# Weight buffers given out by hand, a pair's last product in another place, gates multiplied in two turns, and spilled values read into their own tiles, in a two-layer encoder kernel

## The chip, the cores and the metric

The kernel runs on one core of one Trainium2 chip. The metric is device time in microseconds (us) of one execution of the whole program: the median of three runs, beside one further execution that the hardware profiler recorded.

## What is computed

The reference is a two-layer encoder trunk in fp32 (512 frames of 1024 features). Cut to what matters:

```python
for i in range(2):
    h = rmsnorm(x, norm1_g[i])
    z = h @ w_in[i] + b_in[i]                       # 1024 x 12296, cut into q/k/v/gates
    # branch A: 4 mLSTM heads (dk = dv = 256), q/k through a causal conv and silu
    # branch B: 4 retention heads (dk = 256, dv = 512), rotary q/k, a decay per head
    y_m = sigmoid(mo) * head_layernorm(mlstm(...))
    y_r = silu(rg) * head_layernorm(retention(...))
    merged = sigmoid(gm) * (y_m @ w_bm[i]) + sigmoid(gr) * (y_r @ w_br[i])
    x = x + merged @ w_out[i]
    x = x + square(relu(rmsnorm(x, norm2_g[i]) @ w_ff1[i] + b_ff1[i])) @ w_ff2[i] + b_ff2[i]
    x = x + sigmoid(rmsnorm(x, norm3_g[i]) @ w_pe_gate[i]) * (p[i] @ w_pe[i])
return rmsnorm(x, final_g)
```

## The kernel before

**Number format and matmuls.** Activations are held transposed, features on the 128 partitions and the 512 frames along the free axis. Every operand is split into a high and a low part (`split`, L285): ScalarE (ACT) copies the fp32 value into the reduced format, VectorE (DVE) subtracts that copy from the value. A product of two operands is three TensorE (PE) matmuls: high by high, high by low, low by high. So each weight block of 128x1024 values costs one DMA into a raw buffer (`wr`), one ACT copy (`wh`, L286) and one DVE subtraction (`wl`, L287) before PE can use it.

**Units.** The weights come as one list of units in a fixed order (`unit_list`, L151). A `T8` unit is one 1024x128 block (24 matmuls of 512 columns, `t8`, L446). A `V` unit is a block of a value projection. `PE` units are the two halves of the embedding weights (24 matmuls each, L1443). A `PAIR` is a 1024x256 block that is multiplied with seven products of quarter-size blocks instead of eight (`run_pair`, L472); a `WIDE` is the same for the retention values (`run_wide`, L508). The layer runs through the mLSTM heads, the retention heads 0 to 3, the branch outputs, `w_out`, the first and second feed-forward product (`ff1`, `ff2`, L1363 and L1391) and the gated embedding.

**A pair's seven products.** P1, P5, P6, P2, P3, P7 and P4 are twelve matmuls of 256 columns each. They use three PSUM banks: P1, P6, P7 and P4 are accumulated one after the other in bank `a`, P5 and P3 in bank `c`, P2 in bank `b`. After each product the bank is read out (`done`), by ACT or DVE in `pair_tiles` (L541), by DVE additions into the residual `x` in `ff2` (L1400). P6 can't begin before P1's reading of bank `a` is over, P7 not before P6's, and P4 not before P7's. The weights of a pair are four pieces: A (P1, P5), C (P3, P7), B (P6, P2) and D (P4); D is formed on DVE from the raw pieces (L421 and L424). The last product, P4, is not issued with the other six: it is put into a list `later`, and `flush` (L467) issues it inside the next piece of work. In `run_pair` that is after the next pair's P1 and P5 (L503), in `t8` after half of the block (L454), and there are calls in `scores` (L757), in `attend` (L785) and in `r_out` (L1109). P4's reading then starts what hangs on the pair (`consume`): rotary for the queries and keys, silu for the gates.

**Raw buffers.** There are four raw buffers of one pool tag (`RAWS`, L57), handed out in turn by the pool, and one more in the layer's `low` pool, which is used while units before `w_out` are loaded (`fill_raws`, L362). A raw A piece is kept until C has been split, because D needs both. SyncE (SP) issues the loads in the order of the units.

**Norms.** A norm collects its sum of squares in one tile (`ssum`, L631) and spreads the reciprocal root over the partitions in another (`rb`, L703); both are 512 values wide and sit in the pool `one`.

**Retention heads.** `rv_vals` (L1152) computes the values of two heads at once; those of the second head are written to DRAM. `rv_load` (L1192) brings them back: GpSimd (POOL) issues four loads of 256 KB into temporary tiles (six of them turn round), and ACT and DVE split each into the head's value tiles. `r_gates` (L1091) computes two of a head's four gate tiles as one pair; `r_out` (L1100) transposes the head's output in four steps of four matmuls (`back`, L799) and multiplies each by its gate. `back` needs the scaled output of the head, and the multiplication needs the gate's silu.

**What sets the order.** The program is written in the order above, but a scheduler reorders the instructions within each engine by its own estimate of when operands are ready. So the order on PE is not always that of the code; the order of the built programs was compared for this text. Two kinds of instruction keep the written order: the splits of the weights on ACT and DVE, and the loads on SP. POOL's queue also carries 1 MB DRAM-to-DRAM sums of weight blocks (`step`, L326), each tied to a matmul as a pace.

In the names of the trace `l0r2o1` is layer 0, retention head 2, the second pair of gates; `brq` and `brk` are queries and keys; `l0o31` is block 3, column pair 1 of `ff2` in layer 0; a last letter a, b or c is the PSUM bank.

Of the kernel before, what the change touches and what calls it, by code (L numbers as in the profile page):

```python
# [42 lines left out]
P = 128  # L43
# [191 lines left out]

def build(ctx, tc, ins, out):
# [118 lines left out]
    room = unit_list(0).index(("T8", "w_out", 0, 0))  # L355
    cur["room"], cur["more"] = (), None

# [3 lines left out]

    def fill_raws(most=RAWS + 1):  # L362
        while at["load"] < len(loads) and len(raws) + len(kept) < most:
            n, x = loads[at["load"]]
            r = None
            if n in cur["room"] and cur["more"] not in raws:
                cur["more"] = n, x
                r = cur["low"].tile([P, UN], F32, name=f"wr{at['load']}", tag="wrx", bufs=1)
            elif len(raws) - (cur["more"] in raws) >= RAWS:
# [20 lines left out]
    def prep_next():  # L390
        n, x = order[at["prep"]]
        at["prep"] += 1
        fill_raws()

        w = Q if x == "D" else UN
# [21 lines left out]
        if x == "A" or wide and x[0] == "t2":  # L417
            kept[n, x] = r
        elif x == "C":

            ve.tensor_tensor(raws[n, "B"][:, Q:], kept.pop((n, "A"))[:, Q:], r[:, :Q], OP.add)  # L421
        elif x == "B":

            ve.tensor_tensor(r[:, :Q], r[:, :Q], r[:, Q:], OP.add)  # L424
            formed[n, "D"] = r
        elif wide and x[0] == "B21":
            t = cur["br"].tile([P, UN], F32, name=f"t4{n}_{x[1]}", tag=("ph", "pl")[x[1]])
            ve.tensor_tensor(t, kept.pop((n, ("t2", x[1]))), r, OP.add)
            formed[n, ("t4", x[1])] = t

    def ready(k):
# [39 lines left out]

    def run_pair(name, act, done):  # L472

# [66 lines left out]

    def pair_tiles(name, act, consume, y=None):  # L541

        y = y or [tmp(f"{name}y{d}") for d in range(2)]
        a, b = slice(0, S), slice(S, T)
# [17 lines left out]

        run_pair(name, act, done)

# [37 lines left out]
    class Norm:  # L602


        def __init__(self, name, i, gain, act=None, j0=0, j1=NT):
# [20 lines left out]
        def square(self, k, x, add=None):  # L626
            w = self.n * P
            x = x[:, self.s]
            if self.sum is None:
                pl = cur["last"] if self.half else opool  # L630
                sq = pl.tile([P, w if self.half else T], F32, name=f"{self.name}sum", tag="ssum", bufs=1)[:, :w]  # L631
            else:
# [57 lines left out]
        def spread(self):  # L690
# [10 lines left out]
            te.matmul(o[:, :w], ones_r, dl, start=False, stop=True)  # L701
            pl = cur["last"] if self.half else opool
            self.b = pl.tile([P, w if self.half else T], F32, name=f"{n}rb", tag="rb", bufs=1)[:, :w]  # L703
            ac.activation(self.b, o[:, :w], AF.Copy)
# [71 lines left out]
    def attend(nm, pt, vh, vl, c0, n, num):  # L776
        ph, pl, offs = pt
        for j in range(NT):
# [121 lines left out]
    cur["tmp"], cur["ntmp"] = cur["low"], NTMP  # L900
    cur["room"] = range(room)
    n1 = Norm("l0n1", 0, "g1", acts(xa_pool, "l0n1"))
# [16 lines left out]
    for i in range(L):  # L919
        act_side, ph_side = ("right", "left") if i == 0 else ("left", "right")  # L920
        xa = n1.act
        if i:
            cur["low"] = phase(f"low{i}", ph_side)
            cur["tmp"], cur["ntmp"] = cur["low"], NTMP
            cur["room"] = range(i * NU // L, i * NU // L + room)
        cur["br"] = phase(f"br{i}", ph_side)
# [163 lines left out]

        def r_gates(h, w, gs):  # L1091

# [4 lines left out]

            pair_tiles(f"l{i}r{h}o{w}", xs, consume)

        def r_out(h, num, y, gs=None):  # L1100
            nm = f"l{i}r{h}o"
            if gs is None:
                gs = {}
                r_gates(h, 0, gs)
            r_gates(h, 1, gs)
            for v in range(4):
                o = back(nm, num, v)
                if v == 0:
                    flush()  # L1109
                ve.scalar_tensor_tensor(gs[v], o, bcol(i, "grn", 4 * h + v), gs[v], OP.mult, OP.mult)  # L1110
                split(gs[v], y[0][(4 * h) % 8 + v], y[1][(4 * h) % 8 + v])

        def gm_gates(p):
# [77 lines left out]

        def rv_load(h):  # L1192

            v = value_tiles(f"l{i}r{h}")
            for j in range(NT):
                t = tmp(f"l{i}r{h}vr{j}")
                gp.dma_start(t, rv_dram[i, h // 2, j])
                split(t, v[0][j][:, :T], v[1][j][:, :T])
            return v

        ym = acts(cur["br"], f"l{i}ym")
# [189 lines left out]
        def ff2(b, p):  # L1391
# [10 lines left out]
            def done(x_, o):  # L1402
# [35 lines left out]
        n3_pool = phase(f"n3{i}", act_side)  # L1438
        n3 = Norm(f"l{i}n3", i, "g3", acts(n3_pool, f"l{i}n3"))


        pe = n3_pool.tile([P, KT, T], F32, name=f"l{i}pe", tag="pe")
        for u in range(2):  # L1443
            _, wh, wl = unit("PE")
            for c in range(4):
                o = ps(f"l{i}pe{u}{c}")
                for k in range(2):
                    s = slice((2 * c + k) * P, (2 * c + k + 1) * P)
                    mm3(o, wh[:, s], wl[:, s], pth[:, k, :], ptl[:, k, :], k == 0, k == 1)
                ac.activation(pe[:, 4 * u + c, :], o, AF.Copy)  # L1450
        for _, b, p in rest:
            ff2(b, p)
        flush()
        shift(cur["ff"], ph_side, False)
# [9 lines left out]
        nn = ([Norm(f"l{i}n4{a}", i, "gf", None, 2 * a, 2 * a + 2) for a in range(2)] if last  # L1464
              else [Norm(f"l{i + 1}n1", i + 1, "g1", acts(xa_pool, f"l{i + 1}n1"))])

# [203 lines left out]
```

## Time and profile before

| | us |
|---|---|
| median of three runs (lowest, highest) | 2348.12 (2347.74, 2348.28) |
| the profiled execution's own time | 2347.49 |
| its span, first to last instruction | 2345.8 |
| ScalarE (ACT) busy | 1218.9 |
| GpSimd (POOL) busy | 245.7 |
| DMA: bytes moved | 394.89 MB |

PE is busy for almost the whole span, so the table alone says little. The views that do are the one of waits (who waited for whom, with the length of each wait), the timeline (each instruction with its start, its duration, and in brackets the idle time of its engine before it and what ended that) and the one of one tile. A PE duration in the timeline is that of one matmul from its first to its last step; matmuls overlap, so the pace is read from one start to the next.

### The profile page before, as it was taken

Reading aid. Unit: us, or ns where it says so; the run is one execution under the profiler, and the core shown is the slowest. Engines: PE = TensorE matmul, PEld = TensorE weight load, DVE = VectorE, ACT = ScalarE, POOL = GpSimd, SP = SyncE. Lnnn points to the kernel's source line nnn. Section 1 sums busy time; section 2 is a strip of 40 time slices with the busy share of each in tenths; the row PEclk is TensorE's granted clock in tenths of the full one; section 3 lists DMA queues with packets and bytes.
Section 4 is the critical chain, followed back from the end, with each engine's and each line's share of the span. In section 5 each row is a group of like instructions: output and inputs, shape, how many; then the busy total and the mean of one; then the engine's idle time right before and its main releaser. Section 6 shows DMA issues by size and latency. Waiting matters only on the chain. (4 is left out here: it accounts for less than half of the span.)

```text
span 2345.8 us, 35261 instructions
## 1 busy us (share of the span) xinstructions
PE 2320.2 (99%) x13660; PEld 2056.2 (88%) x13660; DVE 1722.9 (73%) x2658; ACT 1218.9 (52%) x1768; POOL 245.7 (10%) x369
## 2 busy tenths in 40 slices
PE   9999999999999999999999999999999999999998
PEld 7888899898898898899888888998989988998997
DVE  7878767895675577677878787778958656776785
ACT  6656444553554445446557564454536445445454
POOL 3111101100102100000321110000000020000012
PEclk9999999999999999999999999999999999999999
DMA  5666676667578667676775645434343542433431
GB/s 201 187 180 172 218 229 170 205 189 202 168 230 269 195 198 189 199 219 181 206 221 169 182 124 186 136 126 158 108 158 104 166 153 96 130 108 98 132 117 59
DMA packets 146631, 394.89 MB, mean 168 GB/s; under 512 B 15376, under 2 KB 18832, under 8 KB 146464
## 3 DMA queue, kind: packets, MB, share of 16 engines
q1 hardware_dynamic: 99952, 247.77, 32.0%
q0 software_dynamic: 31104, 117.45, 20.4%
q10 hardware_dynamic: 15408, 27.43, 3.3%
q8 instruction: 107, 1.75, 0.3%
q14 instruction: 60, 0.49, 0.1%
HBM read 373.71 MB, written 123.73 MB: 212 GB/s over the span
## 5 line engine op out<-in xcount | busy, mean ns | idle before, releaser
L286 ACT ACTIVATE wh<-wr 128x1024 fp32r<-128x1024 f32 (+1 forms) x223 | 232.2, 1044 | 276.5 <-issue 69.6
L287 DVE TENSOR_TENSOR wl<-wr,wh 128x1024 fp32r<-128x1024 f32 (+1 forms) x221 | 271.9, 1232 | 77.7 <-ACT wh L286 77.5
L286 ACT ACTIVATE wh_B<-wr 128x1024 fp32r<-128x1024 f32 x100 | 105.9, 1059 | 159.2 <-PE l0f L443 8.5
L287 DVE TENSOR_TENSOR wl_B<-wr,wh_B 128x1024 fp32r<-128x1024 f32 x100 | 121.9, 1219 | 32.5 <-ACT wh_B L286 32.3
L286 ACT ACTIVATE wh_D<-wr 128x512 fp32r<-128x512 f32 x76 | 48.0, 632 | 124.9 <-DVE wr L424 65.4
L286 ACT ACTIVATE wh_C<-wr 128x1024 fp32r<-128x1024 f32 x76 | 80.2, 1056 | 61.3 <-issue 9.2
L286 ACT ACTIVATE wh_A<-wr 128x1024 fp32r<-128x1024 f32 x76 | 79.9, 1052 | 54.7 <-PE l1f L443 9.0
L287 DVE TENSOR_TENSOR wl_C<-wr,wh_C 128x1024 fp32r<-128x1024 f32 x76 | 94.3, 1240 | 18.7 <-ACT wh_C L286 18.5
L287 DVE TENSOR_TENSOR wl_A<-wr,wh_A 128x1024 fp32r<-128x1024 f32 x76 | 92.7, 1220 | 17.3 <-ACT wh_A L286 17.3
L442 PE MATMUL l1f<-l1n2h,wh 128*128 128x512 f32 x256 | 99.8, 390 | 0.0
L442 PE MATMUL l0f<-l0n2h,wh 128*128 128x512 f32 x256 | 99.8, 390 | 0.0
L444 PE MATMUL l0f<-l0n2h,wl 128*128 128x512 f32 x256 | 99.7, 389 | 0.0
L444 PE MATMUL l1f<-l1n2h,wl 128*128 128x512 f32 x256 | 99.7, 389 | 0.0
L443 PE MATMUL l1f<-l1n2l,wh 128*128 128x512 f32 x256 | 99.6, 389 | 0.0
L443 PE MATMUL l0f<-l0n2l,wh 128*128 128x512 f32 x256 | 99.6, 389 | 0.0
L287 DVE TENSOR_TENSOR wl_D<-wr,wh_D 128x512 fp32r<-128x512 f32 x76 | 52.4, 689 | 33.2 <-ACT wh_D L286 31.7
L421 DVE TENSOR_TENSOR wr<-wr,wr 128x512 f32<-128x512 f32 x76 | 52.1, 686 | 14.6 <-DMA wr<-wpairs 13.1
L444 PEld LDWEIGHTS l0f<-l0n2h,wl 128*128 128x128 f32 x256 | 48.0, 188 | 10.2
L444 PEld LDWEIGHTS l1f<-l1n2h,wl 128*128 128x128 f32 x256 | 48.1, 188 | 10.1
L443 PEld LDWEIGHTS l1f<-l1n2l,wh 128*128 128x128 f32 x256 | 48.1, 188 | 9.8
L442 PEld LDWEIGHTS l0f<-l0n2h,wh 128*128 128x128 f32 x256 | 48.1, 188 | 9.8
L442 PEld LDWEIGHTS l1f<-l1n2h,wh 128*128 128x128 f32 x256 | 48.1, 188 | 9.7
(5625 smaller groups left out, 8357.9 us busy)
## 6 DMA issues: line engine op xcount, KB each, us to landing
wr<-wstream SPq DMA_DIRECT2D x219, 512.0 KB, 4.2
wr<-wpairs SPq DMA_DIRECT2D x228, 256.0 KB, 2.8
wr<-wwide SPq DMA_DIRECT2D x24, 512.0 KB, 4.0
s0t<-wwide POOLq DMA_DIRECT2D x5, 1024.0 KB, 7.8
s4t<-wwide POOLq DMA_DIRECT2D x5, 1024.0 KB, 9.0
s12t<-wwide POOLq DMA_DIRECT2D x5, 1024.0 KB, 8.1
s16t<-wwide POOLq DMA_DIRECT2D x5, 1024.0 KB, 8.5
s1t<-wpairs POOLq DMA_DIRECT2D x4, 1024.0 KB, 6.7
```

The source lines that it names most:

```text
L286: a = ac.activation(hi_ap, src, AF.Copy)
L287: return a, ve.tensor_sub(lo_ap, src, hi_ap.bitcast(F32))
L421: ve.tensor_tensor(raws[n, "B"][:, Q:], kept.pop((n, "A"))[:, Q:], r[:, :Q], OP.add)
L442: te.matmul(o, sh, mh, start=first, stop=False)
L443: te.matmul(o, sh, ml, start=False, stop=False)
L444: cur["mm"] = te.matmul(o, sl, mh, start=False, stop=last)
```

## The change

Four things are changed.

1. `fill_raws` keeps its own list of free raw buffers. Each has a name and a tag of its own, is taken by a load when it is free, and goes back to the list when the split (or the forming of D) that reads it last has been issued. Beside the four and the one in `low` there is a sixth, `one`: the two norm tiles become one tile `nr` of 1024 values, sum in the first half and spread root in the second, and loads from the unit `WIDE rv0` up to `w_out` may use that tile.
2. `run_pair` calls `flush` after P6 instead of after P5, except in one pair (`early`). The `flush` in `scores` goes, that in `attend` comes after the second block instead of the first. One of the two embedding units is moved behind the last four pairs of `ff2`, with a `flush` in its third block. In `ff2` the norm's `tile3` for the first column tile of a pair is called after P3 instead of P6.
3. `r_out` transposes and multiplies gates 0 and 1 inside the second gate pair (after its P2), transposes 2 and 3 after it, and puts their multiplications into `later`, behind the P4 they need.
4. `rv_load` becomes `rv_fetch`, which loads straight into the low halves of the head's value tiles before the next head's pairs, and `rv_split`, which splits them in place after the scores.

```diff
@@ unit_list
     pairs(ff_order()[0])
     u.append(("PE", 0))
+    pairs(ff_order()[1])
     u.append(("PE", 1))
-    pairs(ff_order()[1])
@@ build
-    cur["room"], cur["more"] = (), None
+    wide0 = unit_list(0).index(("WIDE", (0, "rv0"), 0))
+    where = {n + i * NU // L: ("low", "one") if n >= wide0 else ("low",) for i in range(L) for n in range(room)}
+    free, taken = ["low", "one"] + list(range(RAWS)), {}
+    def norm_tile():
+        return opool.tile([P, 2 * T], F32, name="nr", tag="nr", bufs=1)
+    def raw_tile(a):
+        if a == "one":
+            return norm_tile()
+        pl, tag = (cur["low"], "wrx") if a == "low" else (wpool, f"wr{a}")
+        return pl.tile([P, UN], F32, name=f"wr{at['load']}", tag=tag, bufs=1)
...
+            fits = where.get(n, ()) if n * L // NU == cur["layer"] else ()
+            a = next((a for a in free if a in range(RAWS) or a in fits), None)
+            if a is None:
                 break
-            raws[n, x] = r = r or wpool.tile([P, UN], F32, name=f"wr{at['load']}", tag="wr", bufs=RAWS)
+            free.remove(a)
+            taken[n, x] = a
+            raws[n, x] = r = raw_tile(a)
...
+        def give(*a):
+            free.extend(taken.pop(k) for k in a)
@@ run_pair
-        product("P1")
-        product("P5")
-        flush()
-        for x in ("P6", "P2", "P3", "P7"):
+        for x in ("P1", "P5", "P6", "P2", "P3", "P7"):
             product(x)
+            if x == ("P5" if early else "P6"):
+                flush()
+            if x == "P2" and mid:
+                mid()
         later.append(last)
@@ scores
-        flush()
@@ attend
-            if j == 0:
+            if j == 1:
                 flush()
@@ r_out
-            r_gates(h, 1, gs)
-            for v in range(4):
-                o = back(nm, num, v)
-                if v == 0:
-                    flush()
+            def gate(v, o):
                 ve.scalar_tensor_tensor(gs[v], o, bcol(i, "grn", 4 * h + v), gs[v], OP.mult, OP.mult)
                 split(gs[v], y[0][(4 * h) % 8 + v], y[1][(4 * h) % 8 + v])
+            def turn(a):
+                return [(v, back(nm, num, v)) for v in (a, a + 1)]
+            r_gates(h, 1, gs, mid=lambda: [gate(*t) for t in turn(0)])
+            o = turn(2)
+            later.insert(0, lambda: [gate(*t) for t in o])
@@ rv_load -> rv_fetch, rv_split
-                t = tmp(f"l{i}r{h}vr{j}")
-                gp.dma_start(t, rv_dram[i, h // 2, j])
-                split(t, v[0][j][:, :T], v[1][j][:, :T])
+                gp.dma_start(v[1][j][:, :T].bitcast(F32), rv_dram[i, h // 2, j])
             return v
+        def rv_split(v):
+            for hi, lo in zip(*v):
+                split(lo[:, :T].bitcast(F32), hi[:, :T], lo[:, :T])
@@ order of the retention heads
         num = r_attend(0, pt, vv)
+        vv = rv_fetch(1)
         gs = {}
         r_gates(0, 0, gs)
-        vv = rv_load(1)
         pt = r_scores(1, qk)
+        rv_split(vv)
...
-        r_gates(1, 0, gs)
+        r_gates(1, 0, gs, early=True)
...
         num = r_attend(2, pt, vv)
+        vv = rv_fetch(3)
         qk = r_qk(3)
...
-        vv = rv_load(3)
         pt = r_scores(3, qk)
+        rv_split(vv)
@@ ff2 and the embedding
-                if b == 3 and p and x_ in ("P6", "P7"):
+                if b == 3 and p and x_ in ("P3", "P7"):
...
+        embed(0)
         for _, b, p in rest:
             ff2(b, p)
-        flush()
+        embed(1)
```

More of the change, by code (lines that the diff above doesn't have):

```diff
@@ L355, in build, with fill_raws @@
     room = unit_list(0).index(("T8", "w_out", 0, 0))
[L356 removed]
+    wide0 = unit_list(0).index(("WIDE", (0, "rv0"), 0))
[8 more added lines that the diff above has]
+        return pl.tile([P, UN], F32, name=f"wr{at['load']}", tag=tag, bufs=1)
     def halves(n):
         return [slice(0, Q), slice(Q, UN)] if n == 1 else [slice(0, UN)]
[L362 to L363 removed]
+    def fill_raws(most=None):
+        while at["load"] < len(loads) and at["load"] != most:
             n, x = loads[at["load"]]
[L365 to L369, printed above, removed]
+            fits = where.get(n, ()) if n * L // NU == cur["layer"] else ()
+            a = next((a for a in free if a in range(RAWS) or a in fits), None)
+            if a is None:
                 break
[L371 removed]
+            free.remove(a)
+            taken[n, x] = a
+            raws[n, x] = r = raw_tile(a)
             if x:
@@ L539, in run_wide, with pair_tiles @@
                     done(x, t, bank[b][t])
-    def pair_tiles(name, act, consume, y=None):
-        y = y or [tmp(f"{name}y{d}") for d in range(2)]
+    def pair_tiles(name, act, consume, **kw):
+        y = [tmp(f"{name}y{d}") for d in range(2)]
         a, b = slice(0, S), slice(S, T)
@@ L629, in square @@
             if self.sum is None:
-                pl = cur["last"] if self.half else opool
-                sq = pl.tile([P, w if self.half else T], F32, name=f"{self.name}sum", tag="ssum", bufs=1)[:, :w]
+                if self.half:
+                    sq = cur["last"].tile([P, w], F32, name=f"{self.name}sum", tag="ssum", bufs=1)
+                else:
+                    self.own = self.own or norm_tile()
+                    sq = self.own[:, 0:w]
             else:
@@ L701, in spread @@
             te.matmul(o[:, :w], ones_r, dl, start=False, stop=True)
-            pl = cur["last"] if self.half else opool
-            self.b = pl.tile([P, w if self.half else T], F32, name=f"{n}rb", tag="rb", bufs=1)[:, :w]
+            self.b = self.own[:, T:T + w]
             ac.activation(self.b, o[:, :w], AF.Copy)
@@ L900, in build @@
     cur["tmp"], cur["ntmp"] = cur["low"], NTMP
-    cur["room"] = range(room)
+    cur["layer"] = 0
     n1 = Norm("l0n1", 0, "g1", acts(xa_pool, "l0n1"))
@@ L924, in build @@
             cur["tmp"], cur["ntmp"] = cur["low"], NTMP
-            cur["room"] = range(i * NU // L, i * NU // L + room)
+            cur["layer"] = i
         cur["br"] = phase(f"br{i}", ph_side)
@@ L1089, in r_attend, with r_gates @@
             return num
-        def r_gates(h, w, gs):
+        def r_gates(h, w, gs, **kw):
             def consume(g):
@@ L1438, in build, with embed @@
         n3_pool = phase(f"n3{i}", act_side)
-        n3 = Norm(f"l{i}n3", i, "g3", acts(n3_pool, f"l{i}n3"))
+        n3 = Norm(f"l{i}n3", i, "g3", acts(n3_pool, f"l{i}n3"), own=n2.own)
         pe = n3_pool.tile([P, KT, T], F32, name=f"l{i}pe", tag="pe")
-        for u in range(2):
+        def embed(u):
             _, wh, wl = unit("PE")
@@ L1463, in build @@
         cur["tmp"], cur["ntmp"] = phase(f"pg{i}", ph_side), 7
-        nn = ([Norm(f"l{i}n4{a}", i, "gf", None, 2 * a, 2 * a + 2) for a in range(2)] if last
-              else [Norm(f"l{i + 1}n1", i + 1, "g1", acts(xa_pool, f"l{i + 1}n1"))])
+        nn = ([Norm(f"l{i}n4{a}", i, "gf", None, 2 * a, 2 * a + 2, n3.own) for a in range(2)] if last
+              else [Norm(f"l{i + 1}n1", i + 1, "g1", acts(xa_pool, f"l{i + 1}n1"), own=n3.own)])
         def pe_evac(o, c, s, nn):
```

19 lines of the change are left out of this document (14 added, 5 removed).

## The prediction

> **What bounds the kernel now.** First the page: its first part, then the view of stages for one stretch.
>
> ```profile
> span 2345.8 us, 35261 instructions
> PE 2320.2 (99%) x13660; PEld 2056.2 (88%) x13660; DVE 1722.9 (73%) x2658; ACT 1218.9 (52%) x1768; POOL 245.7 (10%) x369
> ...
> 600.00:660.00 60.00, 56.02 (x422) 53.85 (x421) 46.13 (x75) 37.26 (x63) 2.88 (x4) 0.94 0.50 158
> ```
>
> PE is busy for 2320.2 of 2345.8 us. The change takes no matmul away and adds none, so it can only win what PE loses: 25.6 us of idle time at most, plus time in which matmuls run slowly. Of the stretches of 60 us that I read, the one from 600 stands out inside the kernel: 56.02 us busy, and a granted clock (the last column but two) of 0.94. So the next view is what PE waited for.
>
> ```profile
> PE l0r2o1a L491 <- ACT wh_A L286: 3.4, 1, 3.4
> PE l1o33a L491 <- DVE l1x L1400: 1.6, 1, 1.6
> PE l0o33a L491 <- DVE l0x L1400: 1.3, 1, 1.3
> ...
> PE l0r0o0a L491 <- DVE l0r0o0y L558: 1.2, 1, 1.2
> PE l1r0o0a L491 <- DVE l1r0o0y L558: 1.2, 1, 1.2
> ...
> PE l0r1brqa L491 <- DVE l0r1brqy L558: 1.0, 1, 1.0
> ...
> PE l0o12a L491 <- DVE l0x L1400: 0.7, 1, 0.7
> ...
> PE l1r2o0a L491 <- ACT l1r2o0y L548: 0.5, 1, 0.5
> ...
> PE l0r2o0a L491 <- ACT l0r2o0y L548: 0.4, 1, 0.4
> PE l1r2o1a L491 <- DVE l1r2o1y L558: 0.3, 1, 0.3
> PE l0r2o1a L491 <- DVE l0r2o1y L558: 0.2, 1, 0.2
> ```
>
> There are few waits, each with one place. I sort them by the edit that touches them. Seven are a P4 that waits for P7's reading of bank a by DVE: the two o33, the two r0o0, r1brq and the two r2o1 (6.8 us). Three belong to the values read back in front of r2o0 (3.4 + 0.4 + 0.5 = 4.3 us). The rows left out belong to the first projection, to r0's values and to both ends of the kernel, places where both programs have the same order; they stay, as does the wait at o12, which is a P6.
>
> **What the large wait costs.** The timeline of PE, then of ACT, around it:
>
> ```profile
> 599.98 0.28 PE L492 MATMUL l0r2o0b<-l0xnl,wh_B 128*128 128x256 f32 x1
> 600.10 0.28 PE L493 MATMUL l0r2o0b<-l0xnh,wl_B 128*128 128x256 f32 x1
> 603.78 0.58 PE L491 MATMUL l0r2o1a<-l0xnh,wh_A 128*128 128x256 f32 x1 [3.40 <-ACT wh_A L286]
> ...
> 604.38 0.41 PE L491 MATMUL l0r2o1c<-l0xsh,wh_A 128*128 128x256 f32 x1
> 604.59 0.41 PE L492 MATMUL l0r2o1c<-l0xsl,wh_A 128*128 128x256 f32 x1
> ...
> 609.15 0.33 PE L493 MATMUL l0r2o0c<-l0xsh,wl_C 128*128 128x256 f32 x1
> ```
> ```profile
> 601.16 0.63 ACT L286 ACTIVATE l0r3vh<-l0r3vr 128x512 fp32r<-128x512 f32 x1 [0.48 <-DMA l0r3vr<-rv_spill]
> 602.16 0.63 ACT L286 ACTIVATE l0r3vh<-l0r3vr 128x512 fp32r<-128x512 f32 x1 [0.37 <-DMA l0r3vr<-rv_spill]
> 602.69 1.04 ACT L286 ACTIVATE wh_A<-wr 128x1024 fp32r<-128x1024 f32 x1
> 604.95 0.36 ACT L548 ACTIVATE l0r2o0y<-l0r2o0a 128x256 f32<-128x256 f32 x1
> ```
>
> Matmuls of 256 columns start 0.12 us apart (599.98, 600.10). From 600.10 to 603.78 there are 3.68 us, 3.56 more than that step, so a wait costs 0.16 more than its row says. After it the step is 0.21 (604.38, 604.59) up to 609.15: 5.4 us, less r2o0's wait of 0.4 + 0.16, hold some 23 matmuls that each lose 0.09, 2.1 us. The cause is on ACT: the weight split wh_A that PE needs stands behind value splits that wait for their DMA.
>
> **The sum: what goes.** Part 4 takes the value splits out of this place: in the built program they stand on ACT right behind the outputs of head 2, ahead of the branch output's 192 matmuls (44 us at 0.23 a matmul, two fences on), and the splits of r2o0's weights follow each other. 4.3 us of waits, 3 x 0.16, and 2.1 of slow clock: 6.9 us. Part 2 puts more work between P7 and P4: P6 of the next pair (1.4 us at 0.12 a matmul) for r1brq, the next pair's P1 and P5 for r0o0, attend blocks for r2o1, and 18 embedding matmuls for o33 (4 us). Each is longer than the wait it covers. 6.8 us and 7 x 0.16: 7.9 us. Together 14.8 us.
>
> **What comes, 1: values split earlier.** rv_fetch(1) issues its loads as head 0's value tiles come free, and in the built order two of the four splits stand on ACT ahead of head 0's last output, the third ahead of a key split and of P1's reading in r0o0. The nearest rows are the same loads of before:
>
> ```profile
> 402.92 0.39 PE L444 MATMUL l0r0a<-l0r0vh,l0r0pl 128*128 128x512 f32 x1
> 403.15 0.28 PE L491 MATMUL l0r0o0a<-l0xnh,wh_A 128*128 128x256 f32 x1
> ```
> ```profile
> 405.16 1.27 POOL L1197 DMA_DIRECT2D l0r1vr<-rv_spill  x2 [20.78 <-DVE l0r0mv L792]
> ...
> 408.59 0.59 POOL L1197 DMA_DIRECT2D l0r1vr<-rv_spill  x1
> ...
> 411.51 0.63 ACT L286 ACTIVATE l0r1vh<-l0r1vr 128x512 fp32r<-128x512 f32 x1 [0.41 <-DMA l0r1vr<-rv_spill]
> ```
> ```profile
> DMA to landing us min/median/max: 2.9/3.4/3.7
> ...
> DMA to landing us min/median/max: 4.4/11.1/12.1
> ```
>
> The last two lines are from the views of the tiles l0r1vr and l0r3vr. From issue (408.59) to the waiting split (411.51) there are 2.9 us; I take 3.0. The third tile is read last by the 26th of 30 attend matmuls, which starts four steps of 0.23 before the last (402.0) and ends 0.39 later; issue 402.45, landing 405.45, split to 406.0, key split to 406.55, P1's reading (0.4) to 407.0, P6 at 407.15. PE would come to P6 at 403.15 + 24 x 0.12 and three interleaved matmuls, 406.45. That is 0.7 us late, in two layers: 1.4. Bounds: 0 if the landing is 0.7 us shorter, and 2 x 1.5 with the median landing of 3.4 and both splits behind it; 11 us is a rival below. At head 3 only two splits stand ahead of P1's reading, and the same count ends before P6: 0. The Trainium skill, "DMA: Bandwidth & Descriptors", section "Anatomy of one DMA — SWDGE (gpsimd) path", puts one such transfer at about 2.0 us fixed plus bytes over 436 GB/s, an estimate of 2.6 us for 256 KB. The rows here are above it; by the rule this item would be 0.6 instead of 1.4.
>
> **What comes, 2: P6 in P4's place.** P6 lost the cover that P4 gave it; it waits for P1's reading. In `pair_tiles` ACT reads within 0.5 us and PE needs 1.4 for P5, so nothing is due. In `ff2` the reading is on DVE, behind wl_B. The DVE timeline at o12 and at o32, then PE with the P1 and P6 starts of o32:
>
> ```profile
> 942.25 1.23 DVE L287 TENSOR_TENSOR wl_B<-wr,wh_B 128x1024 fp32r<-128x1024 f32 x1 [2.78 <-ACT wh_B L286]
> 943.39 0.41 DVE L1400 TENSOR_TENSOR l0x<-l0x,l0o12a 128x256 f32<-128x256 f32 x1
> ...
> 1108.35 0.41 DVE L1400 TENSOR_TENSOR l0x<-l0x,l0o31a 128x256 f32<-128x256 f32 x1
> ...
> 1109.28 1.21 DVE L287 TENSOR_TENSOR wl_B<-wr,wh_B 128x1024 fp32r<-128x1024 f32 x1
> 1110.42 0.40 DVE L1400 TENSOR_TENSOR l0x<-l0x,l0o32a 128x256 f32<-128x256 f32 x1
> ```
> ```profile
> 1088.11 0.39 PE L444 MATMUL l0pe<-l0pth,wl 128*128 128x512 f32 x1
> 1088.33 0.28 PE L491 MATMUL l0o30a<-l0hh,wh_A 128*128 128x256 f32 x1
> ...
> 1106.73 0.28 PE L491 MATMUL l0o32a<-l0hh,wh_A 128*128 128x256 f32 x1
> ...
> 1110.97 0.35 PE L491 MATMUL l0o32a<-l0hh,wh_B 128*128 128x256 f32 x1
> ```
>
> P6 starts 4.24 us after P1, and its bank was read 4.09 after P1: just in time. The built order puts seven of P4's twelve matmuls ahead of P6 here, so P6 comes up at 24 + 7 matmuls after P1, 3.67 us, and waits 0.57 for DVE, which goes from P7's reading of o31 to P1's of o32 without a pause. The same for o33, and in layer 1: 2.3 us. I worked the other twenty pairs that have a P4 in front in the same way from their rows. In the pairs 01, 11 and 21 the order leaves P4 first, nothing. At o12 in layer 0 wl_B is late (DVE sat idle 2.78 us for wh_B) and PE waits 0.7 already; with two of P4's matmuls in front instead of twelve it comes 1.2 earlier and waits that much more. o22 there 0.8; the rest 0.5 in all. o31 would wait 0.9 in each layer, but there the built order moves the addition for D, which waited for a DMA, behind the reading; nothing. With half of the embedding gone from the front, o30's hidden tiles have 5.5 us instead of 11; the splits of before end in time, wl_B follows 0.3 late: 0.6 for both layers. Together 5.4 us. Bounds: 0 if DVE's new order makes the readings earlier by as much, 12 if every P6 waits as late as its reading was, with credit only for the pairs 01, 11 and 21.
>
> **What comes, 3: nothing.** The sixth raw buffer and the handing out cost no instruction; `ff2` still has four. Loads come earlier in the retention part, where no wait of PE names one. Shared norm tile: its readers and the loads are far apart. Two-turn gating moves transposes, 16 per head, without adding any; gates 2 and 3 come one P4 later and are used in the branch output, behind 48 matmuls of 0.12 and 18 of 0.23, 9.9 us. Were that cover gone, PE would wait there once per layer for two gate operations and two splits, by the rows of such sizes above 0.6 us each, 2.4.
>
> The sum: -14.8 + 1.4 + 5.4 = -8.0. The profiled execution took 2347.5 us (span 2345.8), so 2339.5; the median of before lies 0.6 higher, which gives **2340.1**.
>
> The Trainium skill, "TensorE: Matmul & The Clock Gate", section "Part 1: The HAM clock gate", says the array falls to half rate after an idle window of about 3.4 us and comes back after about as long a busy one. The trace agrees with the first: of the waits only the one of 3.4 us is followed by slow steps. By the second the slow stretch would cost 1.7 us instead of 2.1, and the sum would be -7.6.
>
> **The rivals.**
> - *Nothing new waits.* DVE's and ACT's new orders absorb the added items: 2348.1 - 14.8 = 2333.3. For it: the scheduler placed P4 first wherever it expected a late reading. Against: its estimates were wrong at the ten waits above. 0.20.
> - *DVE takes it back.* P6 waits in all of `ff2` as the readings of before would make it: -14.8 + 1.4 + 12 = -1.4, 2346.7. For it: DVE has no pause at o32. 0.17.
> - *The change doesn't do what it says at r2o0:* another wait holds ACT there (a score tile that waits for its temporary), and the 6.9 us stay: 2347.0. Against: without the value tiles the six temporaries turn round later. 0.08.
> - *Slower: the loads collide with a 1 MB sum on POOL's queue.* At r3vr of before they took 11 to 12 us that way. Now the splits stand ahead of P1's reading in a pair, so ACT, and PE behind P6, would wait 8.5 us more plus 2.2 of slow clock. At one place of layer 0: -8.0 + 10.7, 2350.8; at both 2361.5. It decides once the landing is 6 us longer than 3.0. Against: POOL had been idle for 20.78 us before the loads of head 1, so no sum was on its way. 0.10.
>
> **How the numbers follow.** My forecast has 0.45, from 2337 to 2343.5. The range must take in the first three rivals and leaves out the fourth and the lowest tail: 2333 to 2348.5. About 0.2% (4.7 us) is what a measurement of this kernel can tell from no change. Faster: 0.45 + 0.20 + 0.07 of the second and third, 0.72. Within: most of those two, 0.16. Slower: the fourth and a tail of the second, 0.12.
>
> **What would show it.** Right: no wait of PE on wh_A at r2o0 and a granted clock of 1.00 there; no P4 among the waits at o33, r0o0, r1brq; new waits under 1 us of P6 on L1400 (renumbered) at o32 and o33, and at r0o0 on ACT behind r1vh. Wrong: waits on rv_spill above 3 us, P6 waits above 1 us in the pairs 12, 13, 22 and 23, or a wait in the branch output.

## The result

The changed kernel takes 2365.78 us (median of six runs, 2362.72 to 2367.81), the kernel before 2348.38 in the same comparison: 1.0072 times as long (95% interval 1.0059 to 1.0085). The forecast was 2340.1, faster; the kernel became slower by 17.4 us. The waits that the change was to remove are gone, but new ones have come, most of them in front of P6, and by the table below they cost more than twice as much.

### The profile page after: what moved, and what is told of

Its sections match the earlier page's. It is cut to its first block, busy times and chain, and to the rows that moved or that the text cites. A ratio compares the mean times of both kernels' runs of the same rounds, so it can differ in the third digit from the quotient of the medians.

```text
span 2363.7 us, 35255 instructions
## 1 busy us (share of the span) xinstructions
PE 2327.3 (98%) x13660; PEld 2060.0 (87%) x13660; DVE 1722.4 (73%) x2658; ACT 1216.3 (51%) x1768; POOL 247.0 (10%) x369
## 3 DMA queue, kind: packets, MB, share of 16 engines
q0 software_dynamic: 31104, 117.45, 20.5%
## 4 chain that ended last, share of the span: by engine, by line
PE 84%; DVE 6%; issue 6%; DMA 2%; ACT 1%; POOL 0%; DVEq 0%; ACTq 0%; POOLq 0%; SPq 0%
PE l1f L462 2%; PE l0f L462 2%; PE l0f L463 2%; PE l1f L463 2%; PE l1f L464 2%; PE l0f L464 2%; PE l1br L462 1%; PE l1br L464 1%; PE l1br L463 1%; DMA wr<-wpairs 1%; PE l0br L462 1%; PE l0br L464 1%; PE l0br L463 1%; DVE wl_B L287 1%; PE l0pg L462 1%
## 5 line engine op out<-in xcount | busy, mean ns | idle before, releaser
L286 ACT ACTIVATE wh<-wr 128x1024 fp32r<-128x1024 f32 (+1 forms) x213 | 220.9, 1042 | 263.8 <-issue 62.2
L287 DVE TENSOR_TENSOR wl<-wr,wh 128x1024 fp32r<-128x1024 f32 (+1 forms) x211 | 258.6, 1227 | 70.1 <-ACT wh L286 69.6
L286 ACT ACTIVATE wh_B<-wr 128x1024 fp32r<-128x1024 f32 x86 | 91.0, 1058 | 113.8 <-DMA wr<-wpairs 10.0
L286 ACT ACTIVATE wh_D<-wr 128x512 fp32r<-128x512 f32 x66 | 41.7, 631 | 150.9 <-DVE wr L441 46.1
L287 DVE TENSOR_TENSOR wl_B<-wr,wh_B 128x1024 fp32r<-128x1024 f32 x86 | 105.1, 1223 | 15.9 <-ACT wh_B L286 15.1
L286 ACT ACTIVATE wh_C<-wr 128x1024 fp32r<-128x1024 f32 x66 | 69.5, 1054 | 48.1 <-PE l0br L463 7.9
L287 DVE TENSOR_TENSOR wl_C<-wr,wh_C 128x1024 fp32r<-128x1024 f32 x66 | 80.6, 1221 | 15.4 <-ACT wh_C L286 15.2
L287 DVE TENSOR_TENSOR wl_D<-wr,wh_D 128x512 fp32r<-128x512 f32 x66 | 45.5, 690 | 46.2 <-ACT wh_D L286 45.7
L463 PEld LDWEIGHTS l0f<-l0n2l,wh 128*128 128x128 f32 x256 | 48.1, 188 | 9.8
```

The lines of the kernel that those rows point to most:

```text
L286: a = ac.activation(hi_ap, src, AF.Copy)
L287: return a, ve.tensor_sub(lo_ap, src, hi_ap.bitcast(F32))
L463: te.matmul(o, sh, ml, start=False, stop=False)
```

## The profile after

First the page's first part. PE executes the same 13660 matmuls, the span is 17.9 us longer, and PE is also counted busy 7.1 us longer.

```profile
span 2363.7 us, 35255 instructions
...
PE 2327.3 (98%) x13660; PEld 2060.0 (87%) x13660; DVE 1722.4 (73%) x2658; ACT 1216.3 (51%) x1768; POOL 247.0 (10%) x369
```

The view of PE's waits (in total, times, longest) is the counterpart of the list that the prediction was built on:

```profile
PE l0gr1a L513 <- DVE wl_B L287: 3.1, 1, 3.1
PE l0o22a L511 <- DVE l0x L1431: 2.7, 1, 2.7
PE l0o12a L511 <- DVE l0x L1431: 1.9, 1, 1.9
PE l1o33a L511 <- DVE l1x L1431: 1.5, 1, 1.5
PE l0r1o0a L511 <- ACT wh_B L286: 1.4, 1, 1.4
PE l1r1o0a L511 <- ACT wh_B L286: 1.4, 1, 1.4
...
PE l0o33a L511 <- DVE l0x L1431: 1.3, 1, 1.3
PE l1o22a L511 <- DVE l1x L1431: 1.1, 1, 1.1
PE l1o12a L511 <- DVE l1x L1431: 1.1, 1, 1.1
...
PE l1r1s L462 <- ACT l1r1kh L286: 0.9, 1, 0.9
PE l1bgm2a L511 <- ACT l1bgm2y L569: 0.8, 1, 0.8
PE l0bgm2a L511 <- ACT l0bgm2y L569: 0.8, 1, 0.8
```

No P4 is among the rows any more, and no wh_A at r2o1: those steps came true. In their place P6 waits, in `ff2` (o12, o22, o33) for P1's reading on DVE, at bgm2 for that on ACT, at r1o0 and gr1 for a split of its own weights. The stretch in which r2o0 and r2o1 now lie runs at full clock, as expected (the last column but two):

```profile
596.00:626.00 30.00, 30.00 (x229) 28.82 (x228) 23.36 (x38) 18.25 (x31) 0.57 (x1) 1.00 0.59 175
```

For a table of where the time went I took each matmul's time from its start to the next start, less the median step of its shape, put it down to the matmul that came late, and added these up by stage, both layers together. A head's output gates have a row of their own (r2o), everything else of the head is in the other (r2); bgm and gr are the gate pairs `gm` and `gr` of the two branches. The table holds waits and slow steps alike; the difference of the sums, 18.1 us, is that of the spans within 0.2. "P4 early" and "P4 late" are the experiments 1 and 4 below, "buffers" is experiment 5.

| us lost on PE | before | after | P4 early in after | P4 late in before | buffers in before |
|---|---|---|---|---|---|
| bgm | 1.1 | 3.5 | 1.1 | 3.5 | 1.1 |
| r1 without its gates | 2.0 | 2.7 | 0.5 | 3.3 | 0.5 |
| r0o | 3.1 | 2.8 | 4.5 | 4.4 | 3.1 |
| r1o | 1.0 | 4.0 | 0.5 | 3.3 | 0.9 |
| r2 without its gates, with the values of heads 2 and 3 | 1.7 | 2.9 | 1.9 | 2.7 | 1.7 |
| r2o | 8.6 | 0.4 | 0.3 | 9.1 | 8.9 |
| r3 without its gates | 0.4 | 2.0 | 1.0 | 0.3 | 0.4 |
| r3o | 0.8 | 0.3 | 0.3 | 1.2 | 8.2 |
| gr | 0.4 | 5.3 | 2.4 | 0.5 | 3.9 |
| ff2 | 5.5 | 18.9 | 2.0 | 20.5 | 5.3 |
| embedding and its gate | 0.9 | 0.6 | 0.6 | 4.7 | 0.9 |
| all else | 15.5 | 15.9 | 16.8 | 17.8 | 16.9 |
| sum | 41.1 | 59.2 | 31.9 | 71.1 | 51.9 |

## The experiments

Three theories stood at first or were formed on the way. **Theory 1**: P4 behind P6 costs; what hangs on P4 comes 1.4 us later, and P6 has nothing in front of it while P1's reading is late. **Theory 2**: the raw buffers given out by hand move the loads, and late weights make the waits. **Theory 3** (formed after experiment 5): the scheduler puts the sum of the raw pieces A and C (L437) of the next pair early on DVE, it waits there for a load, and what PE needs stands behind it.

### 1 and 2: P4 early again

In every pair of the changed kernel, and in `ff2` alone:

```diff
-            if x == ("P5" if early else "P6"):
+            if x == "P5":
                 flush()
```
```diff
-            run_pair(f"l{i}o{b}{p}", [parts(k) for k in range(4)], done)
+            run_pair(f"l{i}o{b}{p}", [parts(k) for k in range(4)], done, early=True)
```

> The changed kernel with P4 put back behind the next pair's P5 in every pair; all else as changed. Theory 1 (lost cover: with P4 behind P6, what hangs on P4 comes 1.4 us later and P6 has nothing in front of it while the reading of P1 is late): the waits of P6 at bgm2 (2.7 us in both layers), r1o0 (3.1), r3brq (1.0) and in ff2 (10.9 more than before) go, the wait of r1brq's P4 (1.2) comes back: 2365.8 - 16.5 = about 2349. Theory 2 (the raw buffers given out by hand move the weight loads into the 1 MB sums, and the late weights make the waits): the waits stay, 2362 to 2366.

> The changed kernel with P4 put back behind P5 in ff2 alone. Theory 1 (lost cover): the waits of P6 at o12, o22, o32 and o33 go, 10.9 us: about 2355, and bgm2, r1o0 and r3brq still wait. Theory 2 (loads moved by the raw buffers): 2362 to 2366, with waits on the weights of B left in ff2.

Everywhere: 2338.47 us, 0.9952 of before (0.9939 to 0.9966), 27.3 less than the changed kernel. In `ff2` alone: 2347.04, 0.9995 (0.9986 to 1.0004), 18.7 less. Theory 1 holds and its size was still too small; theory 2 can't carry it, since the buffers are the same. The page and the longest wait of the first:

```profile
span 2336.5 us, 35251 instructions
```
```profile
PE l0gr1a L513 <- DVE wl_B L287: 1.7, 1, 1.7
```

Of the places that the change touches only gr1 is left above 0.8 us, and this version beats both kernels. To see what the place of P4 does to DVE, here is DVE's timeline at o12 in layer 1, first in the changed kernel, then with P4 early in `ff2`:

```profile
2109.64 0.42 DVE L1431 TENSOR_TENSOR l1x<-l1x,l1o11a 128x256 f32<-128x256 f32 x1
2111.49 0.69 DVE L437 TENSOR_TENSOR wr<-wr,wr 128x512 f32<-128x512 f32 x1 [1.42 <-DMA wr<-wpairs]
2112.10 1.22 DVE L287 TENSOR_TENSOR wl_B<-wr,wh_B 128x1024 fp32r<-128x1024 f32 x1
2113.23 0.41 DVE L1431 TENSOR_TENSOR l1x<-l1x,l1o12a 128x256 f32<-128x256 f32 x1
```
```profile
2096.39 1.22 DVE L287 TENSOR_TENSOR wl_B<-wr,wh_B 128x1024 fp32r<-128x1024 f32 x1 [0.56 <-ACT wh_B L286]
2097.53 0.41 DVE L1431 TENSOR_TENSOR l1x<-l1x,l1o12a 128x256 f32<-128x256 f32 x1
2097.86 0.68 DVE L441 TENSOR_TENSOR wr<-wr 128x512 f32<-128x512 f32 x1
2098.46 0.41 DVE L1431 TENSOR_TENSOR l1x<-l1x,l1o12c 128x256 f32<-128x256 f32 x1
2098.80 0.68 DVE L437 TENSOR_TENSOR wr<-wr,wr 128x512 f32<-128x512 f32 x1
```

In the second, wl_B and P1's reading (the line with l1o12a) go first and the sum L437 for the next pair follows. In the first that sum stands in front, waits 1.42 us for its load, and the reading comes at 2113.23. PE's rows of the changed kernel, P1's first matmul and P6's:

```profile
2109.44 0.28 PE L511 MATMUL l1o12a<-l1hh,wh_A 128*128 128x256 f32 x1
...
2113.79 0.36 PE L511 MATMUL l1o12a<-l1hh,wh_B 128*128 128x256 f32 x1 [1.13 <-DVE l1x L1431]
```

So P4's place does two things here: it takes the cover from P6 (two of P4's twelve matmuls are in front of it, ten behind, 1.18 us), and it changes the scheduler's estimates, so that DVE gets another order. At o33 in layer 1 it is another neighbour, the norm's two operations of 1.5 and 1.6 us, that stands in front.

At bgm2 it is what hangs on P4. ACT's timeline of the changed kernel:

```profile
328.87 0.63 ACT L286 ACTIVATE l0r0qh<-l0r0brqu 128x512 fp32r<-128x512 f32 x1
331.32 0.38 ACT L569 ACTIVATE l0bgm2y<-l0bgm2a 128x256 f32<-128x256 f32 x1 [1.82 <-DVE l0r0ql L287]
331.99 0.38 ACT L571 ACTIVATE l0bgm2y<-l0bgm2c 128x256 f32<-128x256 f32 x1 [0.29 <-DVE l0r0brqw L1088]
```

The queries' P4 begins 5.7 us before bgm2's P1 instead of 7.1, so the rotary on DVE ends later, and P1's reading on ACT waits 1.82 us for DVE's subtraction l0r0ql, which isn't even its operand: probably it frees the temporary tile that the reading writes (argued, not tried). At r1o0, the one pair whose own P4 is early, P1's reading on ACT starts only at 498.18, as P5 ends, and the split of B stands behind it; what holds the reading there is not worked out, but experiment 1 takes this loss away too.

### 3: the values alone

Part 4 in the kernel before (the hunks of `rv_fetch`, `rv_split` and their calls, and no others):

```diff
+        vv = rv_fetch(1)
         gs = {}
         r_gates(0, 0, gs)
-        vv = rv_load(1)
         pt = r_scores(1, qk)
+        rv_split(vv)
```

> The kernel before with part 4 alone (values fetched into their own tiles, split after the scores). My step: the 6.9 us at r2o0 go, and 1.9 us come where the key split of r1 stands behind the value splits, as in the changed kernel: 2348.4 - 5.0 = 2343.4. Rival (the value splits cost more than they give, or another wait takes r2o0's place): 2348 or more.

2345.87 us, 0.9988 (0.9979 to 0.9996): a gain of about 2.8 of the 5.0. The large wait is gone; the head of the list shows what takes part of it back:

```profile
PE l0r0o0a L491 <- DVE l0r0o0y L558: 2.0, 1, 2.0
...
PE l1r0o0a L491 <- DVE l1r0o0y L558: 2.0, 1, 2.0
```

The P4 of r0o0 waited 1.2 before and waits 2.0 now, in both layers; on ACT the value splits now stand among the readings of that pair, which is the likely cause (read from the order, not tried). In layer 1 this wait is followed by a stretch at half clock, from 1581.05 to 1584.46, which costs another 1.5 us. And r3 loses 1.0 more, a loss that the changed kernel has too.

### 4: P4 late alone

In the kernel before (the call of the norm's `tile3` after P3 goes with it):

```diff
-        product("P1")
-        product("P5")
-        flush()
-        for x in ("P6", "P2", "P3", "P7"):
+        for x in ("P1", "P5", "P6", "P2", "P3", "P7"):
             product(x)
+            if x == "P6":
+                flush()
```

> The kernel before with P4 behind P6 in every pair and nothing else (the call of the norm's tile after P3 goes with it). Theory 1 (lost cover): the same waits as in the changed kernel at bgm2, r1o0, r3brq and in ff2, 17.7 us, less r1brq's 1.2: about 2365. Theory 2 (loads moved by the raw buffers): 2347 to 2350, since the raw buffers are those of before.

2376.35 us, 1.0121 (1.0107 to 1.0135): 27.7 slower, with the raw buffers of before. That is the mirror of experiment 1 (27.3) and ends theory 2 as the main cause. In the table `ff2` loses 20.5 here and 18.9 in the changed kernel. The expected 17.7 less 1.2 was too low: the embedding's gate lost 3.8 more, 1.6 of it in a stretch at half clock, and r1 lost 1.3 more instead of gaining.

### 5: the raw buffers alone

Part 1 in the kernel before (`fill_raws`, `prep_next`, `Norm`).

> The kernel before with part 1 alone (raw buffers given out by hand, a sixth one, one shared norm tile). My step: nothing waits for a load where they come earlier, so 2348.7, within 1 us. Rival (the loads now fall into the 1 MB sums): a wait of P6 at gr1 for wl_B in layer 0, as in the three kernels with these buffers (1.7 to 3.1 us), 2350.5 to 2353.

2356.35 us, 1.003 (1.0019 to 1.0041), 8.0 slower: the rival, and more. The waits, and DVE's timeline at r3o1:

```profile
PE l0r2o1a L511 <- ACT wh_A L286: 4.4, 1, 4.4
PE l0r3o1a L511 <- DVE l0r3o1y L578: 3.4, 1, 3.4
PE l0gr1a L513 <- DVE wl_B L287: 2.4, 1, 2.4
PE l1r3o1a L511 <- DVE l1r3o1y L578: 2.1, 1, 2.1
```
```profile
649.65 0.42 DVE L576 TENSOR_TENSOR l0r3o1y<-l0r3o1c,l0r3o1y 128x256 f32<-128x256 f32 x1
653.50 0.69 DVE L437 TENSOR_TENSOR wr<-wr,wr 128x512 f32<-128x512 f32 x1 [3.43 <-DMA wr<-wpairs]
654.11 0.42 DVE L578 TENSOR_TENSOR l0r3o1y<-l0r3o1a,l0r3o1y 128x256 f32<-128x256 f32 x1
```

With one buffer more the scheduler puts the sum L437 of the next pair ahead of P7's reading (L578), for which P4 waits. On the chip the sum waits 3.43 us for its load, which is under way beside a 1 MB sum (s9t, issued on POOL's queue at 640.84). This is where theory 3 comes from.

### 6: the rest of part 2 alone

One embedding unit behind the last pairs, `flush` in the third block of both units, no `flush` in `scores`, that in `attend` after the second block; in the kernel before:

```diff
     pairs(ff_order()[0])
     u.append(("PE", 0))
-    u.append(("PE", 1))
     pairs(ff_order()[1])
+    u.append(("PE", 1))
...
     def scores(nm, qh, ql, kh, kl, decay):
-        flush()
```

> The kernel before with the rest of part 2 and without the move behind P6: one embedding unit behind the last pairs of ff2 with the flush in it, no flush in scores, that of attend after the second block. My steps: the P4 waits at o33 (3.3), r0o0 (2.8) and r2o1 (0.8) go, o30 waits for wl_B (0.9): 2348.7 - 6.0 = 2342.7. Rival (the waits move on to another product): 2347 or more.

2345.35 us, 0.9986 (0.9977 to 0.9995): 3.0 less, half of what was expected. The two o33 gave what the sum said. The two waits at r0o0 went too, but r0o as a stage lost 3.1 before and loses 2.9: P6 and P3 of r0o1 now wait for their readings on ACT instead. The rival was right there.

### 7 and 8: the best version with the old buffers, and with one pair late

Experiment 1 with part 1 taken back; and experiment 1 with

```diff
-            r_gates(h, 1, gs, mid=lambda: [gate(*t) for t in turn(0)])
+            r_gates(h, 1, gs, late=h == 0, mid=lambda: [gate(*t) for t in turn(0)])
```

where `late` keeps `flush` behind P6.

> The changed kernel with P4 early in every pair (2338.5 in its first run) and the raw buffers of the kernel before. If the sixth buffer brings nothing but the wait at gr1: that wait goes, 2336.5. If earlier loads carry part of what that kernel gains: 2340 or more.

> The changed kernel with P4 early in every pair except the second gate pair of head 0, which keeps P4 behind P6. In the first the two waits of that pair's P6 are 0.9 and 0.95 us in each layer, in the changed kernel 0.4 and 0.35: 2 us less, 2336.5. If the difference at this place doesn't come from P4's place: 2338.5.

2337.79 us (0.9953, 0.9940 to 0.9967) and 2337.03 us (0.9951, 0.9938 to 0.9963). Neither differs from experiment 1 by more than the runs of one kernel do. The old buffers lose the wait at gr1 (2.0 less in that stage) and take back r1brq's (1.7 more). In the second the two waits of r0o1 changed (1.16 and 0.29 instead of 0.73 and 0.79) and their sum hardly: the difference at this place did not come from P4's place.

### 9 and 11: the sum held back

The changed kernel, and the version of experiment 1, with the sum bound behind the split of C of its own pair:

```diff
-            ve.tensor_tensor(raws[n, "B"][:, Q:], kept.pop((n, "A"))[:, Q:], r[:, :Q], OP.add)
+            t = ve.tensor_tensor(raws[n, "B"][:, Q:], kept.pop((n, "A"))[:, Q:], r[:, :Q], OP.add)
+            tc.add_manual_dep(t.ins, cur["prep"][1].ins.name, ORDER, reason="sum behind the split of C")
+            cur["prep"] = cur["prep"][0], t
```

> The changed kernel with one order more: the sum of raw pieces A and C (which the scheduler puts wherever it expects its loads) stays behind the split of C of its own pair, so it can't stand on DVE in front of the pair before's wl_B. Theory 3 (where the waits at o12, o22 and gr1 come from: this sum waits on DVE for a load, and wl_B and the reading of P1 wait behind it): these waits go, 1.2 + 1.3 + 4.1 + 4.9 = 11.5 us, about 2354; those of bgm2, r1o0, o32 and o33 stay. Theory 1 alone (P6 has lost its cover and DVE is late anyway): the waits at o12 and o22 stay as long as they are, 2362 to 2366.

> The changed kernel with P4 early in every pair, and the same order for the sum of A and C. Theory 3: the wait at gr1 (1.7) goes with its 2.0 us, about 2336.5. Rival (behind the split of C the sum delays wl_B everywhere): 2340 or more.

2377.03 us (1.0128, 1.0114 to 1.0142) and 2354.82 us (1.0031, 1.0019 to 1.0043): both much slower. For the first neither theory's number came, for the second the rival was right. Where theory 3 named a place it was right: in both kernels the wait at gr1 is gone (that stage loses 1.0 us instead of 5.3, and 0.5 instead of 2.4), and at o12 and o22 in layer 1 P6 no longer waits for DVE's reading (0.3 us for wl_B is left of 1.3). But at o12 and o22 in layer 0 P6 waits about as long as before, 2.0 and 1.7 us, now for ACT's split of B, which waits for the bound sum, and elsewhere more is lost:

```profile
PE l0r1s L464 <- ACT l0r1kh L286: 3.0, 1, 3.0
...
PE l0o12a L513 <- ACT wh_B L286: 2.0, 1, 2.0
PE l0bgm2c L513 <- ACT l0bgm2y L573: 1.8, 1, 1.8
```

```profile
405.44 0.63 ACT L286 ACTIVATE l0r1vh<-l0r1vl 128x512 fp32r<-128x512 f32 x1 [3.85 <-DMA l0r1vl<-rv_spill]
...
949.36 1.06 ACT L286 ACTIVATE wh_B<-wr 128x1024 fp32r<-128x1024 f32 x1 [1.94 <-DVE wr L437]
```

The scores of r1 wait for another reason: in this order the value loads took 4.2 to 5.8 us, and ACT waited 3.85 us for one with the key split behind it. Half clock followed in six places of the first kernel, in which the steps lose about 12 us, against 3 in the changed kernel. So the early sum costs at a few places and gains at the others; the experiment shows the mechanism at the places named, and that binding the sum in this way doesn't pay.

### 12 and 13: the values again, and the two turns

Experiment 1 with `rv_load` in place of `rv_fetch` and `rv_split`; and the kernel before with part 3 alone (`mid` in `run_pair`, `gate` and `turn` in `r_out`).

> The changed kernel with P4 early in every pair, but with the values loaded and split as in the kernel before (part 4 undone). If part 4 carries the gain that its step gave it: the wait at r2o1 and the slow clock (6.9) come back, and the 0.9 us that head 1's and r3's places lost go: 2338.5 + 6.0 = 2344.5. Rival (another edit carries the gain, and the places at r0o and r3brq are worth as much as r2o): 2339 to 2341.

> The kernel before with part 3 alone (a head's gates multiplied in two turns, the last two behind the next P4). My step gave it nothing: 2348.7 within 1 us. What the traces since suggest: the waits of P4 at r2o1 (0.4 in both layers) and r3o1 (0.2) go, 2347.3. Rival (the transposes come later and the branch output or P6 waits): 2350 or more.

2343.86 us (0.9978, 0.9969 to 0.9987): without part 4 the best version is 5.4 slower, against 6.0 expected. Its profile holds more than that: gr loses 5.5 instead of 2.4, since the wait at gr1 is 3.3 us there and half clock follows it; but that execution, with 2347.56 us, is the longest of the eleven. 2348.14 us (1.0003, 0.9994 to 1.0012): the two turns alone are worth nothing, as the prediction had it.

### 14 and 15: the sixth buffer

Part 1 without the sixth buffer, in the kernel before and in the version of experiment 1:

```diff
-    where = {n + i * NU // L: ("low", "one") if n >= wide0 else ("low",) for i in range(L) for n in range(room)}
-    free, taken = ["low", "one"] + list(range(RAWS)), {}
+    where = {n + i * NU // L: ("low",) for i in range(L) for n in range(room)}
+    free, taken = ["low"] + list(range(RAWS)), {}
```

> The kernel before with the raw buffers given out by hand and one shared norm tile, without the sixth buffer. If the sixth buffer is what lets the scheduler put the next pair's sum of A and C in front of P4's reading at r3o1 and of wl_B at gr1: those waits (3.4 + 2.1 + 2.4 and a slow clock) stay out, 2348.5. If the giving out alone does it: 2354 or more.

> The changed kernel with P4 early in every pair, without the sixth buffer. If that buffer makes the wait at gr1: it goes, but the wait of P4 at r1brq (1.2) comes back as in the kernel with the old buffers, 2337.5. If the giving out makes it: 2338.5 with the wait still there.

2349.43 us (0.9997, 0.9988 to 1.0006) and 2338.70 us (0.9951, 0.9938 to 0.9963). Given out by hand, the buffers cost nothing; it is the sixth that makes the waits at r3o1 and gr1. In the best version it is worth nothing: without it gr1 loses 2.0 less and r1 1.7 more.

## Why the prediction was wrong

Its parts, each against what was measured:

- **What goes, 14.8.** r2o0 and r2o1 together: 8.2 gone (8.6 to 0.4), with full clock; expected 4.3 + 0.48 + 2.1, and 0.8 for r2o1's P4, 7.7. The two o33 and r1brq's P4 are gone as well. The 2.7 of r0o0's P4 did not come: as a stage r0o lost 0.4 less, and experiment 6 shows the wait moved on to r0o1.
- **Values split earlier, 1.4.** Measured 1.9 in the changed kernel. The order was the one worked out, but each step came later. ACT's timeline:

```profile
406.02 0.63 ACT L286 ACTIVATE l0r1vh<-l0r1vl 128x512 fp32r<-128x512 f32 x1 [0.31 <-DMA l0r1vl<-rv_spill]
406.56 0.61 ACT L286 ACTIVATE l0r1kh<-l0r1brku 128x512 fp32r<-128x512 f32 x1
407.08 0.36 ACT L569 ACTIVATE l0r0o0y<-l0r0o0a 128x256 f32<-128x256 f32 x1
```

  The working had the split over at 406.0, the key split at 406.55, the reading at 407.0. They are over at 406.65, 407.17 and 407.44; the load had been issued at 402.89 instead of 402.45, and 3.1 us later its split began, where 3.0 was taken. What waits most is the score matmul that needs the key split (0.8 and 1.1 us with the 0.16 that a wait costs on top), not P6. And it waits there only where P4 is late as well: with P4 early r1's scores lose 0.1, and r0o loses 1.7 more instead. At head 3, where the working had 0, r3 loses 1.0 more with the values alone and nothing with P4 late alone.
- **P6 in P4's place, 5.4: the step that failed.** In `pair_tiles` "nothing is due": bgm, r1o and the queries and keys of r2 and r3 lost 2.4 + 3.0 + 1.2 + 1.6 = 8.2 more, of which the 1.6 of r3 belongs mostly to the values, as said. In `ff2` the stage lost 13.4 more although the 3.2 us of o33's P4 went, so 16.6 came, above the bound of 12; 1.1 of it is the faster pace of one stretch before, and 1.5 are slow steps behind the wait at o12 in layer 0 (both in the last section). Both have one error in them: the time of each reading was taken from the rows of before, and only P6 was moved. But the readings stand in a queue, and the same edit moved what stands in front of them: the rotary of a P4 that ends 1.4 later, and the sum L437 by the scheduler's choice. (At r1o0 this is not shown.) The rows of before are no bound for a queue whose order changes. By experiments 1 and 4 the move that this step weighed costs 27 us.
- **Nothing for the sixth buffer: wrong.** That loads come earlier "where no wait of PE names one" was true of before. In the changed kernel gr loses 4.9 more, 1.5 of it in slow steps behind the wait of 3.1 us (below); alone, the buffer costs 8.0 (experiments 5 and 14).
- **Two turns, nothing:** right (experiment 13). **o30, 0.6:** 0.9 measured.

In sum: 8.2 + 3.2 + 1.2 + 0.4 and small ones of 0.8 gone; 1.9 + 8.2 + 16.6 + 4.9 come and 0.4 of small ones: 18.2, beside 18.1 measured.

Of the rivals, "DVE takes it back" named the place, and its 12 us was a bound worked out in the same way as the forecast, so too low. The slower rival had a load that collides with a 1 MB sum. Such collisions happened, but to the weights at gr1 and o22 in layer 0 (sums issued at 659.08 and 1018.60); the value loads that the rival meant landed in time, as the view of head 1's tiles in layer 0 has it (the slowest of the others took 6.2 us):

```profile
DMA to landing us min/median/max: 3.0/3.5/3.9
```

So the rival's sign was right and its mechanism not.

The built orders could have told this: on DVE the sum of the next pair stands ahead of the current wl_B in 32 of 76 pairs before and in 42 after, and o12, o22 and gr1 are among the new ones. In the kernel of experiment 4, with the old buffers, o12 and o22 are among them and gr1 is not; in that of experiment 5, with the new ones, it is the other way round. So P4's place brings the sum forward at o12 and o22, and the sixth buffer at gr1.

## What to carry to other kernels

When an edit moves work between two products that share a bank, don't take the times of the readings from the old trace: walk the reading engine's new queue, and ask of each instruction in front whether it waits for a load or for the work that was moved. A buffer more is not free where a scheduler orders by its own estimates: an operation that it now believes ready goes to the head of an in-order queue, and its load then holds up all that stands behind. And undo the parts one by one: the rest of this change was worth 10 us, and one line of it cost 27.

## What the runs showed of the hardware

**A wait can cost more than itself, and its length alone doesn't say when.** PE's rows at gr1 in the changed kernel, and the window behind the wait:

```profile
673.82 0.28 PE L512 MATMUL l0gr1a<-l0xsl,wh_B 128*128 128x256 f32 x1
677.21 0.38 PE L513 MATMUL l0gr1a<-l0xsh,wl_B 128*128 128x256 f32 x1 [3.11 <-DVE wl_B L287]
...
677.90 0.41 PE L511 MATMUL l0gr1a<-l0xsh,wh_B 128*128 128x256 f32 x1
678.11 0.41 PE L512 MATMUL l0gr1a<-l0xsl,wh_B 128*128 128x256 f32 x1
```
```profile
677.60:681.00 3.40, 3.40 (x18) 3.40 (x18) 2.06 (x4) 2.45 (x4) 0.00 (x0) 0.50 0.08 19
```

The step is 0.21 us instead of 0.12 from 677.68 to 680.88, with a granted clock of 0.50. With P4 early the same wait was 1.7 us and no slow steps followed it: the stage lost 2.9 us less, about half of that by the clock. But at o12 in layer 0 of the changed kernel a wait of 1.9 us was enough, while the wait of 2.7 us at o22 was followed by no slow step:

```profile
945.78 0.35 PE L511 MATMUL l0o12a<-l0hh,wh_B 128*128 128x256 f32 x1 [1.92 <-DVE l0x L1431]
```
```profile
943.80:947.20 3.40, 1.48 (x13) 1.45 (x13) 2.77 (x5) 0.00 (x0) 0.00 (x0) 1.00 0.92 173
947.30:950.70 3.40, 3.40 (x19) 3.40 (x18) 1.42 (x3) 1.24 (x2) 0.00 (x0) 0.50 0.59 117
```

By the trace's record of the granted clock, half clock lasts from 677.63 to 681.04 and from 947.28 to 950.70, 3.41 us each, and from the end of the first to the start of the second there are 78 times that. So the clock seems to change on a fixed grid, and what counts is how much of one stretch of the grid PE was idle: 0.88 of the stretch before the change at gr1 and 0.56 at o12, while at o22 the grid cuts the wait in two, 0.38 and 0.40. In the sixteen traces of this case, the last 13 us of each left out, all 17 stretches at full clock with an idle share of 0.56 or more were followed by half clock, two of the four between 0.50 and 0.55, and one below (experiment 4, at 1153.0).

The Trainium skill, "TensorE: Matmul & The Clock Gate", section "Part 1: The HAM clock gate", has an idle window of about 3.4 us in front of the half rate and as long a busy one behind it. The trace agrees with the second, 3.41 us, and not with the first: at o12 13 matmuls ran in the 3.4 us before half clock.

**Matmuls of 256 columns have two paces at the same granted clock.** In most places they start 0.118 us apart, in some stretches of `ff2` 0.113, as here with P4 early in `ff2`: five steps take 0.57 us.

```profile
2280.38 0.28 PE L511 MATMUL l1o33a<-l1hh,wh_D 128*128 128x256 f32 x1
...
2280.95 0.28 PE L513 MATMUL l1o33a<-l1hh,wl_D 128*128 128x256 f32 x1
```

One such stretch in the same trace has 248 matmuls in 28 us, 1.1 us less than at the other pace, and the granted clock there is 1.00 like everywhere around it. The stretches lie elsewhere in each trace; the changed kernel's has none. What sets the pace stays open.
